# Filling projections in single steps, and the low weights of decay and rate over all rows

## The chip, the cores and the metric

The kernel runs on one core of a Trainium2 chip. The time is the device time of one execution in microseconds (us). A core has four engines that compute: TensorE (PE in the rows; its weight loads are PEld), VectorE (DVE), ScalarE (ACT) and GpSimd (POOL); SyncE (SP) and ScalarE issue most DMAs. Every engine works through its own queue in order and waits where a result of another engine is missing.

## What is computed

One step of a streaming encoder layer, for 1024 new prompt rows and 64 sample rows of width 1024. One input projection feeds two groups of heads. Group A is differential attention (8 heads, a block-causal mask of 64 rows). Group B is an RWKV-7 recurrence (16 heads of 64), whose decay and learning rate come from a projection of rank 64:

```python
proj = h @ w_in
...
w_log = -jax.nn.softplus(-(w0 + jnp.tanh(wd) @ w_up)) - 0.5
decay = jnp.exp(-jnp.exp(w_log))
a = jax.nn.sigmoid(a0 + ad @ a_up)
...
s = s * w_t + sa * b_t + v_t * k_t          # per row t, s is 64x64 per head
...
out = mix @ w_out
x_new = x + _rms_norm(out, norm_post, NORM_EPS)
```

Both groups are gated, joined and sent through one output projection; keys, values, the recurrent state and the last shifted row are returned as well.

## The kernel before

Matrix products of the projections are done as three products of a high and a low part each: weights and activations are split into a rounded high part (`wh`, `hhi`) and the rest (`wl`, `hlo`), and high by high, high by low and low by high are added in PSUM.

The work is cut into *streams*, Python generators that emit instructions and yield. `Weave` decides whose turn it is: it keeps a clock of its own (`now`, moved by `spend` for work of TensorE), each stream says when it may go on (`yield ns`), and the stream of the lowest rank that is due goes first. This fixes the order in every engine's queue; at run time nothing is chosen.

Group B has 17 units, two for each of 8 head pairs (named 0_0, 0_1, 1_0 ... 7_1 in the rows) and one for the sample rows (None_2). A unit first makes decay and rate (`up` products, L513 and L514, into `m_up`), inverts a triangular matrix per chunk in five levels (`m_ip` L684, VectorE L688, `m_iq` L694, VectorE L698 and L703), and then goes through 8 chunks in a chain, one after another: L804 (`pt`) gives a product that VectorE copies (L818, `gsb`), L821 uses it and VectorE copies the result (L827, L828), L832 (`bkt`) updates the state, and VectorE (L842) makes the next chunk's start of it. Beside the three stand L809 or L824 and L833, which sum the output `y`.

Units have ranks 0 to 16. The *filling* has rank 100 and runs when no unit is due. It is first the input projection, in jobs of 128 columns (`proj_cm`): 32 jobs feed the units (r, k, v, g of the 8 pairs) and 32 the attention (aq, ak, av, ag of 8 heads), plus one for decay and rate. A job has three chunks of 384, 384 and 320 rows, each of 24 matmuls into one PSUM tile `pj`: for each of 8 parts of the inner width the three products, L215, L216, L217. It may be interrupted after every third. Of the attention's jobs at least six are held back for the attention. After them the filling is the output projection (`po`, L1145 to L1147), in groups of four by three matmuls of 512 columns, again interrupted after every third.

The attention's streams have ranks from 0 to 80. Per head, `prep` loads queries, keys, values and the gate, splits them, and per 128 query rows come scores (`s`, L1322 and L1323), maximum, exponential, transposes (`x_wt`) and the sum (`x_o`). Keys and queries of four heads at a time are turned by `rope` (rank above 50), in 8 steps that go through DRAM. What is left of the output projection runs alone behind the attention.

For the `up` products, `xw` holds tanh of the decay's activations: the high part in rows 0 to 63 and the low part in rows 64 to 127; `xa` holds the rate's the other way round. The tile `t` holds w_up and a_up twice, in both row halves, their high parts in `t[:, 0:2]` and their low parts in `t[:, 2:4]`. The first of two matmuls takes the high weights by all 128 rows, the second the low weights by the 64 rows of the high activations.

## Time and profile before

| | |
|---|---|
| median of 3 runs | 1876.28 us (1874.08 to 1876.33) |
| the profiled execution | 1870.95 us |
| its span, first to last instruction | 1869.1 us |
| TensorE busy | 1699.6 us (91%) |
| VectorE busy | 1305.8 us (70%) |
| ScalarE, GpSimd busy | 868.1, 695.4 us |
| granted TensorE clock, mean | 0.975 of full |

A matmul's length in a timeline contains its way through the array; where several follow each other, the distance of their starts tells what one costs. Group B ends at 1236 us of the span, the attention at 1746 us.

### The profile page before, as it was taken

How to read it: one execution, taken by the hardware profiler on the slowest of the kernel's cores; microseconds unless marked ns; L12 is line 12 of the kernel's file. 1: busy time of each engine (PE TensorE's matmuls, PEld its weight loads, DVE VectorE, ACT ScalarE, POOL GpSimd, SP SyncE). 2: the span in 40 equal slices, each digit the busy share in tenths (PEclk: the TensorE clock that was granted, in tenths of full speed). 3: DMA queues.
4: the chain of work that ended last, by engine and by line, in shares of the span. 5: the costliest groups of instructions: out<-in, count | busy, mean ns of one | idle time of the engine just before them, and what ended most of it. 6: DMA issues, size and time to landing. Idle time of an engine off the chain costs nothing. (4 is left out here: it accounts for less than half of the span.)

```text
span 1869.1 us, 34871 instructions
## 1 busy us (share of the span) xinstructions
PE 1699.6 (91%) x12930; PEld 1500.6 (80%) x12930; DVE 1305.8 (70%) x2892; ACT 868.1 (46%) x2155; POOL 695.4 (37%) x866
## 2 busy tenths in 40 slices
PE   6999899999998999999999899977899798889995
PEld 5888888888888888888888789877778676777784
DVE  5568777777778787886875766524687667787336
ACT  5534444344344444444443433323566576676323
POOL 4442333233233323323332421212332356554657
PEclk9999999999999999999999999998999899899998
DMA  4110111321122111110101121345555565443325
GB/s 144 49 55 27 50 48 48 80 82 36 39 72 62 51 44 35 52 38 29 57 26 50 57 62 50 106 118 160 153 156 149 165 155 156 121 131 105 116 87 181
DMA packets 204244, 158.85 MB, mean 85 GB/s; under 512 B 44229, under 2 KB 185194, under 8 KB 204074
## 3 DMA queue, kind: packets, MB, share of 16 engines
q1 hardware_dynamic: 169242, 137.33, 25.5%
q10 hardware_dynamic: 34832, 19.30, 4.0%
q8 instruction: 102, 1.67, 0.4%
q14 instruction: 68, 0.56, 0.1%
HBM read 108.67 MB, written 47.34 MB: 83 GB/s over the span
## 5 line engine op out<-in xcount | busy, mean ns | idle before, releaser
L1348 ACT ACTIVATE e<-s,nb 128x512 f32<-128x512 f32 (+4 forms) x208 | 117.3, 569 | 59.3 <-DVE nb L1332 26.1
L1145 PE MATMUL po<-woh,mxh 128*128 128x512 f32 x288 | 120.3, 419 | 7.1 <-DVE part L1156 5.9
L1147 PE MATMUL po<-wol,mxh 128*128 128x512 f32 x288 | 115.9, 402 | 3.9 <-DVE nb L1337 2.5
L1146 PE MATMUL po<-woh,mxl 128*128 128x512 f32 x288 | 115.5, 401 | 4.2 <-POOL mxl L158 4.2
L1332 DVE TENSOR_REDUCE nb<-s 128x1 f32<-128x512 f32 (+4 forms) x208 | 108.0, 529 | 15.9 <-PE s L1323 14.6
L158 POOL TENSOR_TENSOR mxl<-mxr,mxh 128x512 fp32r<-128x512 f32 (+1 forms) x72 | 88.3, 1231 | 74.9 <-ACT mxh L157 61.8
L811 ACT ACTIVATE sd<-suv,dc 64x64 f32<-64x64 f32 x128 | 44.4, 347 | 154.1 <-DVE suv L842 149.4
L1322 PE MATMUL s<-k,qs 128*128 128x512 f32 (+4 forms) x208 | 78.9, 385 | 22.0 <-ACT k L1249 10.0
L1395 PE MATMUL x_o<-vn,wt 128*128 128x128 f32 (+1 forms) x608 | 88.0, 289 | 10.1 <-DVE wt L1385 5.4
L1395 PEld LDWEIGHTS x_o<-vn,wt 128*128 128x128 f32 (+1 forms) x608 | 81.0, 200 | 18.5 <-issue 5.5
L1156 DVE TENSOR_TENSOR part<-po,part 128x512 f32<-128x512 f32 x72 | 49.5, 688 | 55.6 <-PE po L1147 55.5
L842 DVE SCALAR_TENSOR_TENSOR suv<-cbank,dc,sd 64x64 f32<-64x64 f32 x224 | 63.0, 281 | 33.3 <-PE cbank L832 29.2
L832 PE MATMUL cbank<-suv,bkt 128*128 128x128 f32 x256 | 56.9, 304 | 32.0 <-DVE suv L828 32.0
L832 PEld LDWEIGHTS cbank<-suv,bkt 128*128 128x128 f32 x256 | 41.1, 190 | 45.7 <-DVE suv L828 43.4
L215 PE MATMUL pj_v<-hhi,wh_v 128*128 128x384 f32 (+1 forms) x192 | 70.1, 365 | 6.5 <-DVE mg L416 6.1
L1409 POOL TENSOR_SCALAR ms<-ms 128x1 f32<-128x1 f32 x72 | 18.0, 249 | 150.9 <-ACT osq L1407 150.4
L1323 PE MATMUL s<-k,qs 128*128 128x512 f32 (+4 forms) x208 | 71.5, 358 | 2.4 <-POOL k L1252 1.5
L215 PE MATMUL pj_av<-hhi,wh_av 128*128 128x384 f32 (+1 forms) x192 | 70.2, 365 | 3.0 <-DVE fl_g L939 3.0
L157 ACT CAST mxh<-mxr 128x512 fp32r<-128x512 f32 (+1 forms) x72 | 40.7, 567 | 68.7 <-PE po L1147 29.4
L677 POOL TENSOR_TENSOR ltlo<-lt,lt 64x512 f16<-64x512 f32 x32 | 37.7, 1177 | 93.4 <-ACT lt L665 92.2
L1145 PEld LDWEIGHTS po<-woh,mxh 128*128 128x128 f32 x288 | 55.4, 192 | 20.6 <-DVE part L1156 4.4
L215 PE MATMUL pj_k<-hhi,wh_k 128*128 128x384 f32 (+1 forms) x192 | 67.7, 352 | 4.0 <-ACT raw_k L230 4.0
(533 smaller groups left out, 6189.5 us busy)
## 6 DMA issues: line engine op xcount, KB each, us to landing
mxr<-mixB SPq DMA_DIRECT2D x32, 256.0 KB
wor<-in_w_out SPq DMA_DIRECT2D x64, 128.0 KB
qa<-scr_q SPq DMA_DIRECT2D x32, 204.0 KB
ka<-scr_k SPq DMA_DIRECT2D x32, 204.0 KB
scr_q<-fl_q SPq DMA_DIRECT2D x8, 544.0 KB
scr_k<-fl_k SPq DMA_DIRECT2D x8, 544.0 KB
scr_v<-fl_v SPq DMA_DIRECT2D x8, 544.0 KB
scr_g<-fl_g SPq DMA_DIRECT2D x8, 544.0 KB
```

Source lines behind the costliest of these rows:

```text
L158: gtt(lo, raw, hi.bitcast(F32), op=SUB)
L215: mm(ps[:, :n], hi[:, k, :], hhi[i][:, k, :], start=(k == 0), stop=False)
L832: mm(s, bkt[:, c], suv[:, c], start=True, stop=True)
L842: stt(suv[r, c + 1, h, :] if c < 7 and not smp else to[r], s[r, h * CH:(h + 1) * CH], dc[r, c:c + 1], sd[r], op0=MUL, op1=ADD)
L1145: mm(ps, hi[:, q, :], wh, start=(q == 0), stop=False)
L1146: mm(ps, lo[:, q, :], wh, start=False, stop=False)
L1147: mm(ps, hi[:, q, :], wl, start=False, stop=(q == len(ks) - 1))
L1322: mm(s[:, 0:w], lq, k1[c][:, k0 + o_:k0 + o_ + w], start=True, stop=False)
L1323: mm(s[:, 0:w], lq, k2[c][:, k0 + o_:k0 + o_ + w], start=False, stop=True)
L1332: nc.vector.tensor_reduce(nb[:, i_:i_ + 1], s[:, 0:w], axis=AX.X, op=MAX, negate=True)
L1348: act(e[:, o_:o_ + w], s[:, 0:w], AF.Exp, bias=mx, accum_out=sm)
L1395: mm(ops[:, 0:P], wt[0:w, b, :], vn[0:w, vb, :], start=(b == 0), stop=(b == len(kbs) - 1))
```

## The change

`proj_cm` yields after each of the 24 matmuls instead of each third, and spends a third as much of Weave's clock each time; so does the output projection. The constant `QK`, which was 1, goes, and the start of the program takes three steps of the first job where it took one. In the `up` products the second matmul takes all 128 rows of the low weights and the activations instead of 64, so that the low weights are multiplied by the low activations too. Line numbers move: L215 to L217 are L216 in the changed kernel, L1145 to L1147 are L1147, and L513, L514 stay.

```diff
--- before.py
+++ after.py
@@ -42,7 +42,6 @@
 LA, LAT, W_LD, W_DMA = 130, 100, 11000, 3122
 MB = 3
 W_L0 = 22000
-QK = 1
 DVE, ACT, POOL = "DVE", "ACT", "POOL"
 RS = 1.0
 RATE = {DVE: 1 / 0.96, ACT: 1 / 1.2, POOL: 2.4}
@@ -212,12 +211,12 @@
         for i, (t0, n) in enumerate(TCH):
             ps = pjp.tile([P, 512], F32, tag="pj", name=f"pj_{tag}_{i}")
             for k in range(KC):
-                mm(ps[:, :n], hi[:, k, :], hhi[i][:, k, :], start=(k == 0), stop=False)
-                mm(ps[:, :n], hi[:, k, :], hlo[i][:, k, :], start=False, stop=False)
-                mm(ps[:, :n], lo[:, k, :], hhi[i][:, k, :], start=False, stop=(k == KC - 1))
-                weave.spend(3 * n / 2.4 + 60)
-                if k < KC - 1 and k % QK == QK - 1:
-                    yield 0
+                for j, (a, b) in enumerate(((hi, hhi), (hi, hlo), (lo, hhi))):
+                    last = k == KC - 1 and j == 2
+                    mm(ps[:, :n], a[:, k, :], b[i][:, k, :], start=(k == j == 0), stop=last)
+                    weave.spend(n / 2.4 + 20)
+                    if not last:
+                        yield 0
             evac(ps[:, :n], t0, n)
             yield 0
 
@@ -252,7 +251,7 @@
                 gk = pc(R_NP + k)
                 act(hhi[g][:, k, :], ps[:, :w], AF.Copy, scale=gk)
                 stt(hlo[g][:, k, :], ps[:, :w], gk, hhi[g][:, k, :].bitcast(F32), op0=MUL, op1=SUB)
-                if g > 0 and k % QK == QK - 1:
+                for _ in range(3 if g > 0 else 0):
                     next(first[1])
             if g == 0:
                 raw, evac = raw_rows("wa")
@@ -507,11 +506,12 @@
                     d = op_(POOL, 256)
                 yield d
                 for q, t in enumerate(ups):
-                    for j, (x, r) in enumerate(((xw, slice(0, 64)), (xa, slice(64, 128)))):
+                    for j, x in enumerate((xw, xa)):
                         o_ = pss2[j][:, (q0 + q) * CH:(q0 + q + 1) * CH] if smp else pss2[j]
                         cl = slice(TP, T) if smp else slice(hf * HALF, (hf + 1) * HALF)
+
                         mm(o_, t[:, j], x[:, cl], start=True, stop=False)
-                        mm(o_, t[r, 2 + j], x[r, cl], start=False, stop=True)
+                        mm(o_, t[:, 2 + j], x[:, cl], start=False, stop=True)
                 spend(900)
 
             sq = t512(nm=f"sq{u}")
@@ -1142,12 +1142,12 @@
             ps = pjp.tile([P, 512], F32, tag="pj", name=f"po{g}{tt}{ch}")
             for q, k in enumerate(ks):
                 wh, wl = ws[g][k, ch]
-                mm(ps, hi[:, q, :], wh, start=(q == 0), stop=False)
-                mm(ps, lo[:, q, :], wh, start=False, stop=False)
-                mm(ps, hi[:, q, :], wl, start=False, stop=(q == len(ks) - 1))
-                spend(690)
-                if q < len(ks) - 1:
-                    yield 0
+                for j, (a, b) in enumerate(((hi, wh), (lo, wh), (hi, wl))):
+                    last = q == len(ks) - 1 and j == 2
+                    mm(ps, a[:, q, :], b, start=(q == j == 0), stop=last)
+                    spend(230)
+                    if not last:
+                        yield 0
             p_ = part[tt][:, ch * 512:(ch + 1) * 512]
             if g in (0, 2):
                 nc.scalar.copy(p_, ps)
```

All orders below are TensorE's. Each row is line, operation, output, inputs and size; a number behind a name is a tile's own. The first place is the up products of unit 5_1 (`m_up5_1`), with the filling job av1 (or ag0) and the chain of unit 4_1 around it. Before:

```order
L217 MATMUL pj_av1_0_9238<-hhi0_173,wl_av1_9035 128x384
L513 MATMUL m_up5_10_9262<-xw_466,t_wus5_10_9264 128x512
L514 MATMUL m_up5_10_9262<-xw_466,t_wus5_10_9264 128x512
L832 MATMUL cbank_509<-suv4_1_8924,bkt4_1_8893 128x128
L833 MATMUL y4_10_9006<-suv4_1_8924,rbk4_1_8252 128x128
L513 MATMUL m_up5_11_9263<-xa_467,t_wus5_10_9264 128x512
L514 MATMUL m_up5_11_9263<-xa_467,t_wus5_10_9264 128x512
L215 MATMUL pj_av1_0_9238<-hhi0_173,wh_av1_9034 128x384
```

After:

```order
L216 MATMUL pj_ag0_0_9206<-hhi0_173,wh_ag0_9001 128x384
L513 MATMUL m_up5_10_9220<-xw_466,t_wus5_10_9222 128x512
L514 MATMUL m_up5_10_9220<-xw_466,t_wus5_10_9222 128x512
L513 MATMUL m_up5_11_9221<-xa_467,t_wus5_10_9222 128x512
L514 MATMUL m_up5_11_9221<-xa_467,t_wus5_10_9222 128x512
L216 MATMUL pj_ag0_0_9206<-hlo0_176,wh_ag0_9001 128x384
L216 MATMUL pj_ag0_0_9206<-hhi0_173,wl_ag0_9002 128x384
```

The four stand side by side after the change; before, the chain's L832 and L833 stood between the second and the third, as they did in the second units of pairs 2 to 6.

The second place is one chunk in the chain of unit 4_1, from L804 by L821 (input `gsb4_12`) to L832. Before:

```order
L804 MATMUL cbank_509<-suv4_1_8924,pt1_499 128x128
L809 MATMUL y4_10_9006<-suv4_1_8924,pt1_499 128x128
L215 MATMUL pj_v5_2_9170<-hhi2_175,wh_v5_8795 128x320
L216 MATMUL pj_v5_2_9170<-hlo2_178,wh_v5_8795 128x320
L217 MATMUL pj_v5_2_9170<-hhi2_175,wl_v5_8796 128x320
L215 MATMUL pj_v5_2_9170<-hhi2_175,wh_v5_8795 128x320
L216 MATMUL pj_v5_2_9170<-hlo2_178,wh_v5_8795 128x320
L217 MATMUL pj_v5_2_9170<-hhi2_175,wl_v5_8796 128x320
L821 MATMUL cbank_509<-gsb4_12_9187,xtf_504 128x128
L215 MATMUL pj_v5_2_9170<-hhi2_175,wh_v5_8795 128x320
L216 MATMUL pj_v5_2_9170<-hlo2_178,wh_v5_8795 128x320
L217 MATMUL pj_v5_2_9170<-hhi2_175,wl_v5_8796 128x320
```

After:

```order
L804 MATMUL cbank_509<-suv4_1_8653,pt1_499 128x128
L809 MATMUL y4_10_8702<-suv4_1_8653,pt1_499 128x128
L216 MATMUL pj_r5_0_8759<-hlo0_176,wh_r5_8401 128x384
L216 MATMUL pj_r5_0_8759<-hhi0_173,wl_r5_8402 128x384
L821 MATMUL cbank_509<-gsb4_12_8839,xtf_504 128x128
L216 MATMUL pj_r5_0_8759<-hhi0_173,wh_r5_8401 128x384
L216 MATMUL pj_r5_0_8759<-hlo0_176,wh_r5_8401 128x384
L216 MATMUL pj_r5_0_8759<-hhi0_173,wl_r5_8402 128x384
L216 MATMUL pj_r5_1_8869<-hhi1_174,wh_r5_8401 128x384
L832 MATMUL cbank_509<-suv4_1_8653,bkt4_1_8628 128x128
L833 MATMUL y4_10_8702<-suv4_1_8653,rbk4_1_8055 128x128
L568 MATMUL m_ib5_00_8871<-ident_79,t_inx5_0_8848 128x128 x4
```

Between L804 and L821 stood six filling matmuls and stand two; between L821 and L832 six and four.

The third place is the start of the attention: the transposes of the cached keys (`x_ck`) and the first scores of head 0 (`s0_000`). Before:

```order
L215 MATMUL pj_av4_2_15426<-hhi2_175,wh_av4_15152 128x320
L216 MATMUL pj_av4_2_15426<-hlo2_178,wh_av4_15152 128x320
L217 MATMUL pj_av4_2_15426<-hhi2_175,wl_av4_15153 128x320
L1232 MATMUL x_ck00_15518<-ident_79,ck0_15299 128x128
L1232 MATMUL x_ck01_15527<-ident_79,ck0_15299 128x128
L1322 MATMUL s0_000_15602<-k100_15557,qs00_15544 128x128
L1323 MATMUL s0_000_15602<-k200_15568,qs00_15544 128x128
```

After:

```order
L216 MATMUL pj_ak6_0_15146<-hlo0_176,wh_ak6_15033 128x384
L216 MATMUL pj_ak6_0_15146<-hhi0_173,wl_ak6_15034 128x384
L1232 MATMUL x_ck00_15170<-ident_79,ck0_14961 128x128
L1232 MATMUL x_ck01_15176<-ident_79,ck0_14961 128x128
L216 MATMUL pj_ak6_1_15182<-hhi1_174,wh_ak6_15033 128x384
L216 MATMUL pj_ak6_1_15182<-hlo1_177,wh_ak6_15033 128x384
L216 MATMUL pj_ak6_1_15182<-hhi1_174,wl_ak6_15034 128x384
...
L216 MATMUL pj_ak6_1_15182<-hlo1_177,wh_ak6_15033 128x384
L216 MATMUL pj_ak6_1_15182<-hhi1_174,wl_ak6_15034 128x384
L1322 MATMUL s0_000_15226<-k100_15194,qs00_15184 128x128
L1323 MATMUL s0_000_15226<-k200_15203,qs00_15184 128x128
```

Twelve filling matmuls now stand between the transposes and the first score. From the last instruction of group B (the transpose `shp`) to the first score it is 93 filling matmuls before and 135 after.

## Rows read from the trace of the kernel before

**Rows 1.** The page, part 1: busy time, share and instructions of each engine.

```profile
PE 1699.6 (91%) x12930; PEld 1500.6 (80%) x12930; DVE 1305.8 (70%) x2892; ACT 868.1 (46%) x2155; POOL 695.4 (37%) x866
```

**Rows 2.** Windows: a cycle of group B, and a stretch of the attention.

```profile
core 0: us, PE busy (x) PEld busy (x) DVE busy (x) ACT busy (x) POOL busy (x), PEclk, DMA share, GB/s
...
809.40:938.90 129.50, 123.60 (x1097) 110.93 (x1097) 100.56 (x214) 56.55 (x129) 42.87 (x53) 1.00 0.13 41
1516.00:1682.00 166.00, 147.04 (x846) 119.76 (x844) 131.05 (x323) 113.50 (x336) 89.76 (x108) 0.97 0.53 141
```

**Rows 3.** Waits of PE, 278 to 1067 us: total us, times, longest us.

```profile
PE cbank L832 <- DVE suv L828: 23.0, 29, 3.2
...
PE m_iq L694 <- DVE q L688: 2.6, 6, 0.6
```

**Rows 4.** Timeline of PE, unit 3_0's up matmuls: start, length, instruction.

```profile
417.53 0.47 PE L513 MATMUL m_up<-xw,t_wus 128*128 128x512 f32 x1
417.93 0.50 PE L514 MATMUL m_up<-xw,t_wus 64*128 64x512 f32 x1
418.36 0.50 PE L513 MATMUL m_up<-xa,t_wus 128*128 128x512 f32 x1
418.79 0.50 PE L514 MATMUL m_up<-xa,t_wus 64*128 64x512 f32 x1
419.22 0.45 PE L215 MATMUL pj_r<-hhi,wh_r 128*128 128x384 f32 x1
419.50 0.34 PE L216 MATMUL pj_r<-hlo,wh_r 128*128 128x384 f32 x1
419.68 0.34 PE L217 MATMUL pj_r<-hhi,wl_r 128*128 128x384 f32 x1
```

**Rows 5.** Timeline of PE in the tail: 512-column matmuls over 128 rows.

```profile
1800.16 0.39 PE L1145 MATMUL po<-woh,mxh 128*128 128x512 f32 x1
1800.39 0.39 PE L1146 MATMUL po<-woh,mxl 128*128 128x512 f32 x1
```

**Rows 6.** Line L514, its matmuls of the prompt units: count, shortest, median, longest.

```profile
L514 PE MATMUL m_up<-xw,t_wus x16: 492/502/502, 66.4 to 1076.6; 64*128 64x512 f32 x16
```

**Rows 7.** Timeline of PE: the sample unit's first batch, and four transposes.

```profile
1013.83 0.28 PE L513 MATMUL m_upNone<-xw,t_wusNone 128*128 128x64 f32 x1
...
1017.42 0.44 PE L215 MATMUL pj_av<-hhi,wh_av 128*128 128x384 f32 x1
...
1231.71 0.60 PE L906 MATMUL m_zt<-ident,ycp 128*128 128x128 f32 x4
```

**Rows 8.** Timeline of PE, start of the attention; idle time and releaser in brackets.

```profile
1250.38 0.31 PE L216 MATMUL pj_av<-hlo,wh_av 128*128 128x320 f32 x1
1250.52 0.30 PE L217 MATMUL pj_av<-hhi,wl_av 128*128 128x320 f32 x1
1252.24 0.41 PE L1232 MATMUL x_ck<-ident,ck 128*128 128x128 f32 x2 [1.42 <-DMA ck<-in_cache_k]
1262.67 0.47 PE L1322 MATMUL s<-k,qs 128*128 128x128 f32 x1 [10.02 <-ACT k L1249]
```

**Rows 9.** Timeline of PE and DVE, a chain step of unit 4_1.

```profile
743.30 0.38 PE L804 MATMUL cbank<-suv,pt 128*128 128x128 f32 x2
...
743.67 0.48 PE L651 MATMUL m_bo<-t_kbh,bdr 128*128 128x512 f32 x1
...
743.73 0.29 DVE L818 COPY gsb<-cbank 128x128 f32<-128x128 f32 x1 [0.81 <-PE cbank L804]
...
744.74 0.38 PE L821 MATMUL cbank<-gsb,xtf 128*128 128x128 f32 x2
...
745.68 1.25 DVE L369 SCALAR_TENSOR_TENSOR vs__491<-pv,vs__491 128x1 f32<-128x1 f32 x1
...
747.29 0.23 DVE L828 COPY suv<-cbank 64x64 f32<-64x64 f32 x1
747.57 0.49 PE L832 MATMUL cbank<-suv,bkt 128*128 128x128 f32 x2 [0.74 <-DVE suv L828]
```

## The prediction

> **What bounds the kernel now.** I read the page's busy shares first: TensorE is busy for 1699.6 of 1869.1 us [rows 1], far ahead of the next engine. Then the windows by stage. The kernel has three: the recurrent heads (group B, up to 1236 us) with the projections as filling, the attention (to 1746 us) with the last projections and the output projection as filling, and a tail of output projection alone. In group B the program repeats itself every 129.5 us, one head pair a cycle: in the cycle from 809.4 us TensorE is busy 123.6 of 129.5 us, VectorE 100.6 [rows 2]. In the attention stretch from 1516 us it is 147.0 and 131.1 of 166 us [rows 2]. So TensorE is the bound nearly everywhere, VectorE stands close behind, and the time of the kernel is TensorE's work plus what TensorE waits. The profile shows its waits in group B: between 278 and 1067 us the longest group by far is L832, the chain's state update, which waits 29 times for the copy L828, 23.0 us together and up to 3.2 us at once; the inversion's L694 waits 6 times, 2.6 us together [rows 3].
>
> The change touches both: it takes work from TensorE (the low part), and it moves where TensorE stands when it waits (the interruptions). The number of instructions is the same; only their order and the shape of 48 matmuls differ.
>
> **Part 1, the low part over all rows: -18 us.** Per unit four matmuls of 512 columns: full rows, 64 rows, full rows, 64 rows. In the trace they start at 417.53, 417.93, 418.36 and 418.79 us, the filling follows at 419.22: 1.69 us, some 0.43 us each once the shapes alternate, and the first filling matmul behind takes 0.28 us to its successor instead of 0.18 [rows 4]. Matmuls of 512 columns over 128 rows that follow each other start 0.23 us apart [rows 5]. So what costs is not the columns but the alternation, about 0.2 us at each step. With all four over 128 rows I expect 4 x 0.23 = 0.92 us and no surcharge behind: 1.79 - 0.92 = 0.87 us less per unit, and 16 prompt units [rows 6] make 13.9 us. The sample unit has 32 such matmuls of 64 columns in two batches of 16; a batch takes 1017.42 - 1013.83 = 3.59 us, 0.22 us each [rows 7]. No row shows a 64-column matmul of this type in a stream of its own kind; four 128-column transposes take 0.60 us with their drain [rows 7], so 0.15 us each is an upper bound: 16 x 0.15 = 2.4 us, 1.2 us saved per batch, 2.4 in all, and 7.2 if they cost nothing. Together 16.3 to 21.1; I take 18 us, nearer to the low end since a 64-column row has more overhead than columns. All of it lies on TensorE, which is 95% busy; it covers nothing now, so nothing is uncovered. If VectorE were the bound there, it would come back as idle time (a rival below). The added product (low weights by low activations) costs no instruction: POOL already writes the low weights of all rows (L506).
>
> The Trainium skill, "TensorEngine Tiling (Array Packing)", Key Properties, says that changing the tiling mode drains the engine; the trace agrees with 0.43 against 0.23 us [rows 4, 5]. The same section says that different row tiles can load and multiply in parallel, which speaks against the change: the two 64-row matmuls lie on different row halves and could share one's time, 16 x 0.23 = 3.7 us given up. They start 0.86 us apart with a full-row matmul between [rows 4], so there is nothing to give up; by that rule alone the sum would be 3.7 us worse.
>
> **Part 2, fewer other changes of row shape: -4 us.** In TensorE's order I counted the places where a 64-row matmul stands next to a 128-row one: 486 before, 96 of them at the up projection; 362 after, none of them due to it. The other 390 thus become 362. Such a place costs between 0.10 us (the 0.28 for 0.18) and 0.20 us (0.43 for 0.23) [rows 4]: 28 x 0.15 = 4 us, bounds 3 and 6.
>
> **Part 3, the start of the attention: -7 us.** At 1250.52 us the last filling matmul stands, then TensorE waits 1.4 us for the cache and 10.0 us for the cast of head 0's keys [rows 8]. That cast waits for loads, which start with the stage, not with the filling. Before, 93 filling matmuls stand between group B's last work and the first score, after 135, 12 of them behind the cache transposes (the third place in the order). 42 x 0.16 us, between the 0.18 us of 384 columns [rows 4] and the 0.14 of 320 [rows 8], is 6.7 us of work that now lies in the wait. Bounds: 0, if the loads come later by as much, and 11.4, the whole wait.
>
> **Part 4, the interruptions: +12 us, bounds -5 and +50.** A filling projection has 24 matmuls per chunk; a unit's work could stand behind every third, now behind each. What this does not change is the amount of filling: 4,680 + 864 matmuls. They are interrupted 778 times before and 802 times after, 7.1 and 6.9 matmuls from stop to stop. So the cover of an average step is as it was; it is divided otherwise. Before, 552 of the 778 runs are exactly 3, 6 or 9 matmuls long; after, 545 of 802 are 1 to 5. A step of the chain that got 6 by rounding up now gets 2 to 4, and the rest stands where the unit waits for its projections. Is that still enough? The shortest answer to L804 in the trace: it starts at 743.30, the copy L818 runs from 743.73 to 744.02, so 0.72 us; L804 and its companion L809 take 0.37 us to the next matmul, and two filling matmuls 2 x 0.17 more, 0.71 in all [rows 9]. Just covered. L821 to L832 needs L821's 0.38, two copies of 0.23 and handovers, about 1.0 us [rows 9]; four filling matmuls (the second place) and L821's own slot, half of the 0.37, give 0.9: short by 0.1. But where TensorE waits long now, it waits for VectorE's queue: behind L821 at 744.74 stands an L369 of 1.25 us ahead of the copies, so that they end at 747.52 us and L832 starts at 747.57 after 0.74 us idle, although eight matmuls lay between [rows 9]. Such waits are neither made nor mended by a finer grain. There are 17 units x (24 chain steps + 9 inversion steps) = 561 steps. If a fifth of them lack 0.1 us, as the second example does, that is 11 us; I take 12. Upper bound: one filling matmul, 0.17 us, on half of them, 48, taken as 50. Below nothing: the L832 that stands amid the up projection (the first place) stands elsewhere after, and its 0.74 us, five times over by the same place of five units, would be -4; with the few waits at L694 I call it -5. I take a value near the low end, because the plan knows VectorE's load, and where it leaves little cover today (L694, 6 waits [rows 3]) it waits little.
>
> In the attention the score-to-output order has nearly as many rows from the first score to the last output matmul, 2226 before and 2241 after. I take +3 us there, bounds 0 and the 19 us that TensorE is idle in the stretch of 166 us [rows 2]. With group B shorter in filling, projections move into the attention and output projection out of it: 441 of its matmuls stand behind the attention before, 629 after. These 188 run there at 0.23 us each [rows 5], 43 us of work that is taken from the stages ahead, so moving it costs nothing. With the filling move its weight loads on SP, their splits on ACT and POOL and its evacuations; only the rope below comes close to its use by that.
>
> Sum: -18 - 4 - 7 + 12 + 3 = -14 us on the profiled execution's 1870.95 us (span 1869.1 and 1.85 around it), 1857 us. That execution lies 5.3 us below the median of the three runs; a median is asked for, so 1876.3 - 14 = 1862 us.
>
> **Rivals.** *Late answers outweigh it (slower).* TensorE's queue is in order: a unit's matmul that is put behind one filling matmul instead of three stops all filling when VectorE's copy is not there. Parts 1 to 3 give 29 us; over 802 stops that is 36 ns each, so a mean added wait over 36 ns, a fifth of one filling matmul, turns the sign. For it: 1.0 us needed against 0.9 given at L832, where the longest waits are already; VectorE at 78% in the cycle, rising if the cycle shrinks. Against it: 7.1 and 6.9 matmuls per stop. At the upper bound: 1876.3 - 29 + 50 = 1897 us, with 0.1 us on all 561 steps 1876.3 - 29 + 56 = 1903. In the same case I count the rope of the keys of heads 4 to 7: its last step now stands beside the last scores of head 3, where before it stood at the start of head 2, and a late load would stop the scores of head 4 as it stops head 0 today, 10 us [rows 8]. Chance 0.24.
>
> *VectorE or the chain is the bound in the cycle (same).* Then parts 1 and 2 come back as idle time and parts 3 and 4 cancel: within 4 us of 1876. For it: VectorE's 100.6 of 129.5 us and its in-order queue; against it: TensorE's 123.6. Chance 0.12.
>
> *The units gain and nothing is lost.* Part 4 at its lower bound, part 1 at 22: 1876.3 - 38 = 1838 us. It is the low edge of the forecast's case, which has 0.64 in all.
>
> **How the numbers follow.** Forecast 1862 us, 0.64. A measurement of this kernel tells 0.2%, 3.8 us, from no change. Faster by more: 0.64; within: 0.12; slower: 0.24. The range leaves out one tenth at each side: down to 1842 (part 4 at nothing, part 3 at its bound, attention at 0), up to 1890 (the first rival short of its upper bound).
>
> **What would show it.** Right: the four up matmuls about 0.23 us apart and the cycle about 2 us shorter; the wait for head 0's cast near 3 us; L832's waits in sum as before. Wrong: more TensorE waits of 0.1 to 0.3 us at L821, L832, L694 and L684; a wait at head 4's first score; or a cycle that stays at 129.5 us with VectorE's share as before. If the time falls much below 1842, waits vanish that I hold to be VectorE's own.

## The result and the profile after

The changed kernel takes 1936.19 us (median of 4 runs, 1930.36 to 1937.15), the kernel before 1875.18 in the same comparison: 1.0324 times as long, interval 1.0296 to 1.0353. The change makes the kernel slower by some 61 us. The profiled execution has a span of 1928.6 us where before had 1869.1.

The page of the changed kernel, part 1, answers to [rows 1]; below it, from the view by cores, span and mean granted clock of TensorE (0.975 before):

```profile
PE 1719.9 (89%) x12930; PEld 1510.3 (78%) x12930; DVE 1299.7 (67%) x2892; ACT 866.7 (45%) x2155; POOL 688.8 (36%) x866
```

```profile
core 0: 1928.6 us, clock 0.960
```

The 59.5 us more of span split in two. TensorE idles 208.7 us instead of 169.5, 39.2 more. And it is busy 20.3 us longer, with as many instructions and less work in them: the second part of the loss is the clock, below.

By stage the trace gives: group B ends at 1224.3 us (1235.6 before), 11.3 us earlier with 234 filling matmuls fewer in it; from there to the first score 32.3 us (27.0); the attention 506 us (483); the tail 43 us more, for the 188 output matmuls that the prediction saw move there.

In group B's steady part TensorE has the same instructions in each cycle before and after, 432 of them filling. The windows: the cycle of the changed kernel that answers to [rows 2], then four cycles together, in the changed kernel and in the kernel before.

```profile
core 0: us, PE busy (x) PEld busy (x) DVE busy (x) ACT busy (x) POOL busy (x), PEclk, DMA share, GB/s
705.30:839.80 134.50, 125.52 (x1096) 111.64 (x1095) 100.10 (x216) 56.27 (x128) 41.59 (x53) 0.99 0.13 41
434.80:973.70 538.90, 503.07 (x4380) 447.26 (x4379) 403.03 (x873) 225.24 (x512) 166.70 (x211) 0.98 0.16 47
417.50:939.00 521.50, 495.31 (x4384) 443.78 (x4382) 405.34 (x874) 226.41 (x513) 170.52 (x209) 1.00 0.16 47
```

The cycle is 5.0 us longer, not 2 shorter; VectorE's time in it is unchanged. Of the 17.4 us in four cycles 9.6 are idle time and 7.8 more busy time.

TensorE's waits in the stretch of [rows 3], in the changed kernel: total us, times, longest us.

```profile
PE m_iq L694 <- DVE q L688: 15.8, 7, 3.1
PE cbank L821 <- DVE gsb L818: 11.5, 17, 1.4
PE cbank L804 <- DVE suv L842: 10.7, 16, 1.0
PE m_ip L684 <- DVE x L703: 5.4, 8, 2.3
PE cbank L832 <- DVE suv L828: 5.3, 7, 1.0
```

In the kernel before, beside the rows of [rows 3]:

```profile
PE cbank L821 <- DVE gsb L818: 5.8, 6, 1.8
PE m_ip L684 <- DVE x L703: 0.4, 2, 0.2
```

L832, the longest group before, has fallen from 23.0 to 5.3 us. L694 has grown from 2.6 to 15.8, and L821, L804 and L684, at which the prediction's sum had at most 0.1 us here and there, wait 27.6 us together, where L821 and L684 had 6.2 and L804 was not among the waits. The waits went to the steps that were covered before, or nearly so.

**Where the answer comes late: one chunk.** Timeline of PE and DVE, two chunks of a chain just ahead of the up products of unit 3_0, the place of [rows 4]; idle time and releaser in brackets:

```profile
432.20 0.39 PE L832 MATMUL cbank<-suv,bkt 128*128 128x128 f32 x2
...
432.42 1.26 DVE L966 TENSOR_TENSOR raq<-raq,rbq 128x136 f32<-128x136 f32 x1
...
433.17 0.34 PE L216 MATMUL pj_r<-hhi,wh_r 128*128 128x384 f32 x1
433.71 0.60 DVE L842 SCALAR_TENSOR_TENSOR suv<-cbank,dc,sd 64x64 f32<-64x64 f32 x2
434.37 0.49 PE L804 MATMUL cbank<-suv,pt 128*128 128x128 f32 x2 [0.86 <-DVE suv L842]
...
434.83 0.48 PE L513 MATMUL m_up<-xw,t_wus 128*128 128x512 f32 x1
435.15 0.39 PE L514 MATMUL m_up<-xw,t_wus 128*128 128x512 f32 x1
435.38 0.40 PE L513 MATMUL m_up<-xa,t_wus 128*128 128x512 f32 x1
435.62 0.39 PE L514 MATMUL m_up<-xa,t_wus 128*128 128x512 f32 x1
```

Between L833 and L804 stand four filling matmuls, some 0.7 us. The answer L842 stands on VectorE behind a rope step of 1.26 us (L966), and TensorE is idle for 0.86 us. Before, six stood at this place and sixteen small products of an inversion (L694), and L804 did not wait. The last four rows show part 1 as forecast: 0.23 us apart behind the first.

**And what a wait costs behind it.** TensorE and VectorE, an inversion level of the changed kernel:

```profile
616.86 0.34 PE L216 MATMUL pj_ak<-hlo,wh_ak 128*128 128x384 f32 x1
...
618.64 0.69 DVE L875 TENSOR_TENSOR ycp<-ycp,gva 128x512 f32<-128x512 f32 x1 [2.05 <-POOL gva L873]
619.25 0.68 DVE L688 TENSOR_TENSOR q<-m_ip,mt 128x512 f16<-128x512 f32 x1
...
619.99 0.63 PE L694 MATMUL m_iq<-xt_a,q 64*64 64x64 f16 x16 [2.79 <-DVE q L688]
...
621.04 0.52 PE L216 MATMUL pj_ak<-hhi,wh_ak 128*128 128x384 f32 x1
621.36 1.05 PE L906 MATMUL m_zt<-ident,ycp 128*128 128x128 f32 x4
```

Windows ahead of, in and behind this wait (columns as above):

```profile
613.00:616.80 3.80, 3.55 (x31) 3.23 (x30) 3.56 (x7) 2.05 (x4) 2.89 (x4) 1.00 0.46 132
616.80:619.90 3.10, 0.40 (x3) 0.08 (x1) 1.26 (x3) 0.00 (x0) 1.96 (x3) 0.82 0.09 21
619.90:624.50 4.60, 4.51 (x31) 4.27 (x32) 2.66 (x6) 1.56 (x3) 2.03 (x2) 0.50 0.00 0
624.50:630.00 5.50, 5.50 (x52) 4.90 (x51) 5.44 (x10) 2.59 (x6) 1.69 (x2) 0.90 0.07 20
```

L688 stands on VectorE right behind L875, which waits 2.05 us for GpSimd; six filling matmuls cover 1.0 us, and TensorE idles 2.79. Then the granted clock is 0.50, the lower of its two levels (1.2 against 2.4 GHz), for 4.6 us, and a filling matmul of 384 columns takes 0.32 us to its successor (621.04 to 621.36) where it takes 0.17 elsewhere. So this wait costs 2.8 us at once and, by an estimate of half the 4.5 busy us at 0.50, 2.3 more behind it. The same wait comes back at 485.87, 757.74 and 891.63 (2.80, 2.79 and 2.79 us), with a granted clock of 0.61 to 0.64 over the 4.2 to 4.8 us from there. Over the whole span busy time by the share of clock not granted is 1719.9 x 0.040 = 69 us after and 1699.6 x 0.025 = 42 us before: an estimate of 26 us for the clock's part in the loss. To be explained are some 32: the 20.3 us of busy time, and the 11.5 by which the low part over all rows shortens it when it stands alone (first experiment). What makes the other 6 is not shown.

### The profile page after: what moved, and what is told of

Same layout as the page of the kernel before. It is cut to its first block, busy times and chain, and to the rows that moved or that the text cites. A ratio compares the mean times of both kernels' runs of the same rounds, so it can differ in the third digit from the quotient of the medians.

```text
span 1928.6 us, 34957 instructions
## 1 busy us (share of the span) xinstructions
PE 1719.9 (89%) x12930; PEld 1510.3 (78%) x12930; DVE 1299.7 (67%) x2892; ACT 866.7 (45%) x2155; POOL 688.8 (36%) x866
## 4 chain that ended last, share of the span: by engine, by line
PE 52%; DVE 20%; POOL 8%; ACT 7%; DMA 6%; issue 5%; ACTq 1%; SPq 1%; POOLq 0%; DVEq 0%
PE po L1147 8%; PE pj_aq L216 4%; PE pj_av L216 4%; PE pj_v L216 3%; PE pj_r L216 3%; PE pj_ak L216 3%; PE pj_k L216 3%; PE pj_g L216 3%; PE cbank L821 2%; PE pj_ag L216 2%; PE cbank L804 2%; PE cbank L832 2%; PE x_o L1395 2%; PE m_s L633 2%; POOL inv L547 1%
## 5 line engine op out<-in xcount | busy, mean ns | idle before, releaser
L1348 ACT ACTIVATE e<-s,nb 128x512 f32<-128x512 f32 (+4 forms) x208 | 117.2, 569 | 63.5 <-DVE nb L1337 32.4
L1147 PE MATMUL po<-woh,mxh 128*128 128x512 f32 x288 | 117.1, 407 | 7.0 <-DVE part L1156 5.9
L1147 PE MATMUL po<-wol,mxh 128*128 128x512 f32 x288 | 116.8, 406 | 0.6 <-POOL wol L157 0.5
L1147 PE MATMUL po<-woh,mxl 128*128 128x512 f32 x288 | 116.0, 403 | 1.1 <-POOL mxl L157 1.1
L1381 PE MATMUL x_wt<-ident,e 128*128 128x128 f32 (+1 forms) x304 | 55.1, 296 | 32.1 <-DVE e L1370 9.4
L842 DVE SCALAR_TENSOR_TENSOR suv<-cbank,dc,sd 64x64 f32<-64x64 f32 x224 | 63.1, 282 | 30.1 <-PE cbank L832 25.7
L1409 POOL TENSOR_SCALAR ms<-ms 128x1 f32<-128x1 f32 x72 | 22.0, 305 | 163.7 <-ACT osq L1407 163.3
L688 DVE TENSOR_TENSOR q<-m_ip,mt 128x512 f16<-128x512 f32 x80 | 55.2, 690 | 30.9 <-PE m_ip L684 29.8
L821 PE MATMUL cbank<-gsb,xtf 128*128 128x128 f32 x256 | 58.5, 310 | 16.5 <-DVE gsb L818 16.3
L1381 PEld LDWEIGHTS x_wt<-ident,e 128*128 128x128 f32 (+1 forms) x304 | 38.2, 149 | 43.7 <-ACT on L1403 10.0
L1147 PEld LDWEIGHTS po<-woh,mxh 128*128 128x128 f32 x288 | 55.5, 193 | 21.2 <-DVE part L1156 4.5
L216 PE MATMUL pj_k<-hhi,wh_k 128*128 128x384 f32 (+1 forms) x192 | 67.4, 351 | 4.3 <-ACT raw_k L229 4.3
L804 PE MATMUL cbank<-suv,pt 128*128 128x128 f32 x256 | 59.0, 313 | 12.9 <-DVE suv L842 12.1
```

Of the source, the lines that this page charges most:

```text
L216: mm(ps[:, :n], a[:, k, :], b[i][:, k, :], start=(k == j == 0), stop=last)
L804: mm(g, pt[:, c, 0:2, :], suv[:, c], start=True, stop=True)
L821: mm(uu, xtf[:, c], gsb, start=True, stop=True)
L842: stt(suv[r, c + 1, h, :] if c < 7 and not smp else to[r], s[r, h * CH:(h + 1) * CH], dc[r, c:c + 1], sd[r], op0=MUL, op1=ADD)
L1147: mm(ps, a[:, q, :], b, start=(q == j == 0), stop=last)
L1348: act(e[:, o_:o_ + w], s[:, 0:w], AF.Exp, bias=mx, accum_out=sm)
```

## The experiments

Intervals are of the ratio to the kernel before, measured beside it. `LAT` (100 ns, group B) and `LA` (130 ns, attention) of line 42 are the planner's allowance: it adds them to the time at which it takes an answer to be there, so they decide how much filling it puts behind a step. A chain step has two such stops: one until VectorE's copy is issued, and one until the next product.

### The three parts alone

**Low part over all rows.**

```diff
-                    for j, (x, r) in enumerate(((xw, slice(0, 64)), (xa, slice(64, 128)))):
+                    for j, x in enumerate((xw, xa)):
...
-                        mm(o_, t[r, 2 + j], x[r, cl], start=False, stop=True)
+                        mm(o_, t[:, 2 + j], x[:, cl], start=False, stop=True)
```

> The kernel before with the low part over all rows alone; the order of all instructions is that of before. Theory A (part 1 of the prediction holds, the loss is all from the finer interruptions): 18 us of TensorE work less, the four matmuls about 0.23 us apart, 1875 - 18 = 1857 us, 1852 to 1862. Rival B (the saved TensorE time comes back as waits, since VectorE or the chain is the bound of a cycle): 1871 to 1876 us, the cycle stays at 129.5 us. Rival C (full rows are dearer than I think and are part of the loss): over 1876 us.

Measured: 1867.77 us, 0.9973 (0.9959 to 0.9987), -5 us: between the theories. The order is that of before. From the first up matmul to the instruction behind the last, the 16 prompt units sum to 24.0 us instead of 32.4; the sample unit's first batch is

```profile
1010.10 0.28 PE L513 MATMUL m_upNone<-xw,t_wusNone 128*128 128x64 f32 x1
...
1011.89 0.42 PE L215 MATMUL pj_av<-hhi,wh_av 128*128 128x384 f32 x1
```

1.79 us instead of 3.59 [rows 7]. The second gains nothing (4.88 us, 4.82 before), and the rows show why: it stands behind a wait of 3.13 us at L832 and runs at a granted clock of 0.50, its matmuls 0.21 us apart instead of the first batch's 0.11, where before no such wait stood ahead of it and it ran at 1.00. The windows of the second batch, here and in the kernel before (columns as above):

```profile
1023.00:1028.00 5.00, 4.37 (x20) 3.83 (x18) 2.35 (x6) 2.33 (x6) 2.71 (x4) 0.50 0.01 2
1026.80:1031.70 4.90, 3.96 (x19) 3.02 (x18) 2.75 (x6) 2.33 (x6) 2.63 (x4) 1.00 0.01 2
```

So 10.2 us are saved, and 1.6 more on the first matmul behind each of the units; TensorE is busy 1688.1 us, 11.5 less than before. More than half comes back as waits: over 66 to 1236 us, where before had 32.0 us at L832 (36 times) and 7.7 at L821 (9 times), this kernel has

```profile
PE cbank L832 <- DVE suv L828: 36.5, 36, 3.2
PE cbank L821 <- DVE gsb L818: 10.9, 13, 1.8
```

**Grain of the input projections.**

```diff
...
-                weave.spend(3 * n / 2.4 + 60)
-                if k < KC - 1 and k % QK == QK - 1:
-                    yield 0
...
+                    weave.spend(n / 2.4 + 20)
+                    if not last:
+                        yield 0
...
```

> The kernel before with the input projections alone interruptible at each matmul; low part over 64 rows, output projection by thirds. Theory A (answers of VectorE come late in group B and in the attention's first half, where these projections are the filling): most of the loss, 1876 + 45 to 65 = 1920 to 1940 us. Rival B (the loss comes from the attention with the output projection as filling): 1876 to 1890 us.

Measured: 1938.02 us, 1.0355 (1.0340 to 1.0371): theory A. It is the whole loss, 65 us, with the cycles of the changed kernel (134.5 us).

**Grain of the output projection.**

```diff
...
-                spend(690)
-                if q < len(ks) - 1:
-                    yield 0
...
+                    spend(230)
+                    if not last:
+                        yield 0
...
```

> The kernel before with the output projection alone interruptible at each matmul. Group B is then as before, word for word. Theory A: the score's and sum's answers come late in the second half of the attention, +5 to +20 us, 1880 to 1895 us. Rival B (the attention's loss in the changed kernel comes from the keys' rope of heads 4 to 7 and from the shifted projections, not from the grain): 1871 to 1879 us.

Measured: 1869.12 us, 0.9987 (0.9972 to 1.0002): no change, against theory A and just below rival B's range. The attention falls from 483 to 470 us, and 44 output matmuls go to the tail, 10 us. The loss in the attention is not from this part.

### Cover given back, and taken away without the grain

**The changed kernel with more allowance.**

```diff
-LA, LAT, W_LD, W_DMA = 130, 100, 11000, 3122
+LA, LAT, W_LD, W_DMA = 310, 280, 11000, 3122
```

> The changed kernel, with two constants of the plan raised by 180 ns each: LAT from 100 to 280 (group B) and LA from 130 to 310 (attention), the time that the plan adds to each answer. 180 ns is half of what a stop came later on average when a third was the grain (half of 540 against half of 180 ns). 4067 filling matmuls then stand in group B (4083 before, 3849 in the change), 493 output projection matmuls behind the attention (441 and 629). Theory A (a finer grain took away a cover that the plan's short answer times needed): the waits at L804, L821, L684 and L694 in group B fall back to the 14 us of before, and the time to 1855 to 1870 us. Rival B (being interrupted so often costs by itself, whatever the cover: row shapes, weight loads, clock): it stays at 1915 us or more. Rival C (the place of the later jobs, the rope of heads 4 to 7 above all, does it): group B recovers half, the attention stays at 500 us or more, 1890 to 1910 us.

Measured: 1875.18 us, 1.0013 (0.9994 to 1.0031). The loss is gone, though every projection can still be interrupted at each matmul (830 interruptions, 802 in the changed kernel), and four cycles take 519.3 us. That is theory A's mechanism, 5 us above its range: the gain of the low part does not come on top, and the waits at its four lines do not fall back to the 14 us of before. From 66 to 1236 us they are 54 us in the changed kernel and 27 here. Waits from 278 to 1067 us:

```profile
PE cbank L832 <- DVE suv L828: 18.3, 17, 3.4
PE cbank L821 <- DVE gsb L818: 8.0, 12, 1.4
...
PE cbank L804 <- DVE suv L842: 6.9, 6, 1.3
PE m_iq L694 <- DVE q L688: 2.9, 3, 1.4
```

Between the kernel before and the changed one it is the division of the same 432 filling matmuls of a cycle that differs. I counted two steps in TensorE's order, for all 17 units:

| filling matmuls | before | changed | more allowance |
|---|---|---|---|
| L804 to L821: mean | 9.9 | 6.2 | 8.6 |
| of 136, with three or fewer | 22 | 67 | 25 |
| L684 to L694: mean | 6.3 | 4.8 | 5.6 |
| of 85, with five or fewer | 14 | 69 | 40 |

**In group B alone (`LAT` 280), in the attention alone (`LA` 310), and half of both (190, 220).**

> The changed kernel with the allowance per step raised from 100 to 280 ns in group B alone; in the attention it stays at 130 ns. The run with both raised took 1875 us, the changed kernel 1936. Theory A (cover is lost in each stage by itself; by the stage times 36 us of the loss stand in group B and 20 to 25 in the attention): 1893 to 1905 us, with group B back near 1230 us. Theory B (the loss in the attention is a consequence of group B, from which 234 filling matmuls were pushed out into it): 1873 to 1883 us. Theory C (the attention is the larger part): above 1912.

> The changed kernel with the allowance raised from 130 to 310 ns in the attention alone; in group B it stays at 100 ns. Theory A (each stage loses by itself): the attention from first score to last output matmul falls from 506 to some 480 us and the time to 1905 to 1918 us. Theory B (the attention's loss comes from the projections that group B pushes into it): 1928 to 1940 us, no change. Group B itself should be as in the changed kernel, 1224 us, in both.

> The changed kernel with both allowances raised half as far (190 in group B, 220 ns in the attention). A dose: if each nanosecond of cover is worth the same, half of the 61 us comes back, 1900 to 1910 us. If only the last bit of cover up to the answer matters and most steps are just short (a threshold), 1875 to 1890 us; if the steps lack more than half of it, above 1915.

Measured: 1886.64 us, 1.0071 (1.0047 to 1.0094); 1929.00, 1.0289 (1.0264 to 1.0314); 1880.54, 1.0044 (1.0029 to 1.0059). Of the 61 us (by the ratios) group B's allowance alone gives back 47, between the two theories. It also takes the attention from 506 to 474 us, of which the filling that no longer stands there (192 input matmuls fewer, 76 output ones more) explains about 13, an estimate at 0.16 and 0.23 us each. The attention's allowance alone gives back 7, too little for theory A and in theory B's range. Half of both gives back 52, as the threshold reading expects: most of what was missing lay within the first 90 ns of a stop. Why the attention loses when group B is thin stays partly open; that more of the input projections are left for it (696 matmuls instead of 504) is seen in the order, but no run moved those alone.

**The kernel before with less allowance** (`LAT` 2, thirds as before).

```diff
-LA, LAT, W_LD, W_DMA = 130, 100, 11000, 3122
+LA, LAT, W_LD, W_DMA = 130, 2, 11000, 3122
```

> The kernel before, still interrupted at thirds only, with the planner's allowance per step of a unit in group B cut from 100 to 2 ns, so that the order puts 117 fewer filling matmuls into group B (3966 where 4083 stood; the changed kernel has 3849). Theory A (what hurts is the missing cover behind the steps, however it is taken away): slower by about half of what the changed kernel loses in group B, 1890 to 1910 us, with more waits at L804, L694 and L684. Theory B (the single-matmul interruptions themselves hurt, by broken runs of filling, and not the amount of cover): 1870 to 1882 us.

Measured: 1912.90 us, 1.0209 (1.0190 to 1.0227): theory A, somewhat over its range. L821 to L832 now has three or fewer filling matmuls 44 times instead of 20, and four steady cycles take 534 us (521.5). From 278 to 1067 us the waits at L821 are 11.9 us (5.8 before), at L694 5.6 (2.6) and at L684 4.7 (0.4); L804, which theory A names too, has 1.2. The fine grain is not needed for a loss.

**Longer durations instead of a longer allowance** (the changed kernel, `RS = 1.2`, by which the planner multiplies work of VectorE, ScalarE and GpSimd).

> The changed kernel with the planner's durations of work on VectorE, ScalarE and GpSimd raised by a fifth, the allowance per step left at 100 and 130 ns. It gives cover by the length of the work that is waited for, where the raised allowance gave the same to every step. Theory A (the plan's durations were too short, and the thirds' rounding made up for it): 1860 to 1880 us, no worse than the raised allowance's 1875. Theory B (what lacked is the handover of each step, which no duration holds): 1885 to 1915 us.

Measured: 1903.52 us, 1.0166 (1.0148 to 1.0184): theory B. It gives back 30 of the 61 us (by the ratios). Longer durations help the steps with long work: L684 to L694, with 512 columns to mask, has five or fewer 33 times instead of 69. L804 to L821, where 128 columns are copied, still has three or fewer 54 times (67).

**More allowance with thirds** (low part over all rows, `LAT` 200).

> The kernel before with the low part over all rows and the allowance in group B raised from 100 to 200 ns, interruptions at thirds; 105 filling matmuls more than before then stand in group B (4188). The full-row form alone took 1868 us. Theory A (its saving came back as waits because cover was missing, and more cover frees it): 1852 to 1863 us, with shorter waits at L832 and L821. Theory B (cover at thirds was enough; what comes back is the chain's own time): 1866 to 1876 us.

Measured: 1894.72 us, 1.0108 (1.0087 to 1.0129), outside both theories. Four cycles take 538 us, with 33 more filling matmuls (some 6 us), and the waits at L832 hardly shrink (30.5 us over 66 to 1236). More allowance is thus no cure in itself. Counted as above, it did not come to every step: L804 to L821 has three or fewer 38 times (22 before) and L821 to L832 31 times (20), while L832 to the next L804 within a chain has 8.3 on the mean instead of 5.4. That this division is the cost is not shown.

### One place, or many

**The order on VectorE.** In the changed kernel L688 stands right behind L875 (at most two others between) in six places, before in none, and with the raised allowance in none. Is that order the loss?

```diff
+            nrm[0] = True
             yield op_(DVE, 512)
...
             yield op_(DVE, 512)
+            nrm[0] = False
...
             for lv in range(1, 6):
+                yield lambda: not nrm[0]
```

> The changed kernel, with a gate: an inversion level's first product (m_ip) is not issued while an output normalisation stands between its sum of squares and its scaling. It takes away one place that comes back in each head pair of the changed kernel: on VectorE the level's masking stands right behind the normalisation's scaling, which waits 2.05 us for GpSimd, and TensorE then idles 2.79 us and goes on at a lower clock. The filling in group B stays thin (3868 matmuls; 3849 in the changed kernel, 4083 before). Theory A (this order on VectorE is most of the longer cycle): the cycle falls from 134.5 us to 129 to 131 and group B is 20 to 30 us shorter, 1905 to 1918 us in all. Theory B (thin cover everywhere is the loss, this place only one of many): the cycle stays above 133 us, 1925 to 1940 us.

Measured: 1926.64 us, 1.0292 (1.0254 to 1.0331): theory B by the time. But the gate did not take all six places away. Three are left (at 349.6, 487.9 and 1031.5 us; the scaling is L878 and the masking L690 here), and the inversion's product has longer waits than in the changed kernel: 4.96 us at 488.61 and 4.42 at 627.30. The counts of the table stay thin (63 of 136, 66 of 85). Waits from 278 to 1067 us (lines are two higher here):

```profile
PE cbank L823 <- DVE gsb L820: 13.5, 13, 3.4
PE m_iq L696 <- DVE q L690: 11.0, 5, 5.0
PE cbank L806 <- DVE suv L844: 8.2, 12, 1.5
PE cbank L834 <- DVE suv L830: 7.9, 9, 2.4
```

So the whole time does not decide between the theories. Two cycles in which the place is gone tell more; here they are together, and the same two in the changed kernel and in the kernel before (columns as above):

```profile
704.70:970.30 265.60, 247.10 (x2197) 220.81 (x2196) 199.64 (x428) 114.06 (x259) 83.99 (x107) 1.00 0.13 40
705.30:973.70 268.40, 251.03 (x2191) 223.24 (x2190) 199.64 (x429) 112.69 (x256) 82.94 (x105) 0.99 0.13 40
679.80:939.00 259.20, 247.28 (x2193) 221.77 (x2192) 201.13 (x427) 113.11 (x257) 85.70 (x105) 1.00 0.13 41
```

A cycle takes 132.8 us without the place, 134.2 with it and 129.6 before. So the place is worth some 1.4 of the 4.6 us that a cycle lost, and theory B is the nearer one. The rest stays as waits at other steps, 7.7 us at L823 alone; that the gate makes none of them is not shown. Without the two waits of 2.79 us TensorE is at full clock and busy 3.9 us less with the same work. The estimate above, 2.3 us of slower work behind each such wait, gives 4.6.

### Whether TensorE's time counts, and the best version

**No low-weight matmuls at all** (the second of each pair left out; that part of the computation is missing).

```diff
-                        mm(o_, t[:, j], x[:, cl], start=True, stop=False)
-                        mm(o_, t[r, 2 + j], x[r, cl], start=False, stop=True)
+                        mm(o_, t[:, j], x[:, cl], start=True, stop=True)
```

> The kernel before without the low-weight matmuls of decay and rate (the second matmul of each pair, 32 of 512 columns and 16 of 64, left out; that part of the computation is missing). It takes from TensorE some 1.2 us per unit and all changes of row shape there, about 22 us in all, where the full-row form alone took about 14 to 18 and gave 5. Theory A (TensorE's time in group B is worth its full length unless a wait needs it): 1851 to 1860 us. Theory B (the chain's answers set the cycle there, so that time taken from this place comes back as waits at L832 and L821): 1862 to 1870 us, no better than the full-row form by more than 4 us.

Measured: 1857.46 us, 0.9929 (0.9907 to 0.9951): in theory A's range, though not at its full length. The up matmuls take some 24 us less of TensorE, group B ends 17 us earlier, and 13 us (by the ratio) to 16 (by the medians) reach the end. Four cycles take 517.2 us instead of 521.5, with 7.0 us less busy time. So the chain alone does not set the cycle: somewhat over half of what is saved comes through, and the rest comes back as waits.

**The two harmless parts together.**

> Two of the three parts of the change: the low part over all rows and the output projection interrupted at each matmul; the input projections at thirds as before. Alone they measured 0.9973 and 0.9987 of the kernel before. If they add up: 0.995 to 0.997, 1863 to 1868 us. If the finer output projection costs cover in the attention as the finer input projections do in group B, or only moves work to the tail: 1868 to 1876 us.

Measured: 1864.27 us, 0.9955 (0.9941 to 0.9969), -8.4 us: the two add up (0.9973 x 0.9987 = 0.9960). This version beats both kernels.

```profile
PE 1686.2 (91%) x12930; PEld 1498.0 (80%) x12930; DVE 1302.0 (70%) x2892; ACT 865.8 (47%) x2155; POOL 691.7 (37%) x866
```

TensorE is busy 13.4 us less than before [rows 1].

## Why the prediction was wrong, step by step

**The bound: right, and not whole.** TensorE's work plus its waits was the right frame, and TensorE's time does count (the run without low-weight matmuls). Missing was that a long wait also slows the work behind it: 39.2 us of idle time came with 20.3 us of busy time.

**Part 1, -18 us: direction right, about 5 us.** The four matmuls stand 0.23 us apart as forecast. But the step multiplied 0.87 us by all units. Measured in the first experiment are 0.53 us on the mean and 0.10 on the first matmul behind, which the 0.87 held too: the first of the four took 0.33 to 0.40 us before, not 0.43, and where the chain's L832 and L833 stand amid the four (five units of the kernel before, as the first place of the order showed) the gain is 0.3 us. The sample unit gave 1.8 us, once, instead of 2.4, since its second batch fell on the lower clock. That makes 11.8 us, and the sentence that the time "covers nothing now" failed for more than half of it: it stood between steps of other units' chains, and came back at L832 and L821.

**Part 2, -4 us: not told apart.** No run separates it.

**Part 3, -7 us: at its bound of 0.** Timeline of the changed kernel, start of the attention:

```profile
1247.06 0.34 PE L216 MATMUL pj_ak<-hhi,wl_ak 128*128 128x384 f32 x1
...
1255.37 1.20 ACT L1249 CAST k<-ka 128x1216 fp32r<-128x1216 f32 x1 [2.33 <-DMA rot_k<-fl_k]
1256.63 0.47 PE L1322 MATMUL s<-k,qs 128*128 128x128 f32 x1 [9.23 <-ACT k L1249]
```

The wait for head 0's cast is 9.23 us, 10.02 before [rows 8], where the prediction expected near 3. The 42 matmuls more did not lie in the wait; the stage became 5.3 us longer, nearly their 6.7 us. The loads came later by as much, the case that the lower bound held. The first load of the keys, before and in the changed kernel:

```profile
1253.97 0.37 SPq L1206 DMA_DIRECT2D ka<-rot_k  x1
1248.75 0.30 SPq L1206 DMA_DIRECT2D ka<-rot_k  x1
```

It is issued 18 us behind the end of group B before and 24 us after, so the loads do not start with the stage. What holds them is not shown.

**Part 4, +12 us: this step failed.** The input projections' grain costs 65 us by itself. The working was: as many matmuls per interruption (7.1 and 6.9), hence the cover of an average step is as it was. The first half is right: each steady cycle has 432 filling matmuls before and after. The second is not, because a wait is not paid by the average. L804 to L821 lost 3.7 matmuls on the mean, and the steps with three or fewer went from 22 to 67 of 136; what they lost stands between the chain of one unit and that of the next, where the prediction had put it ("where the unit waits for its projections"): from a unit's last L832 to the next unit's first L804 it is 960 filling matmuls in all instead of 639. Within the chains L832 to L804 has about as much as before, 6.0 on the mean and 5.4. The prediction looked at L804 to L821 once, found 0.71 us given and 0.72 needed, and called it covered; a distribution counted in the order would have shown it. The rounding up to thirds was a hidden allowance of about 0.17 us at each stop, an estimate: half of three matmuls against half of one, at 0.17 us each. The runs with `LAT` and `LA` agree: put back, the loss is gone; taken from the kernel with thirds, a loss is there.

Two reasons in that step fell. That waits behind VectorE's queue "are neither made nor mended by a finer grain" is contradicted by L832 (23.0 to 5.3 us) and by L694 and L804, whose new waits stand behind L875 and L966 in that queue. And the upper bound of 50 us took one filling matmul on half of the steps, with no room for the clock.

**Attention, +3 us: 23 measured.** The waits from the first score to the last output matmul grew, at changing lines; idle time there is 78 us instead of 57, at a clock of 0.92 instead of 0.95. The windows after and before (columns as above):

```profile
1257.00:1762.00 505.00, 426.92 (x2560) 369.30 (x2560) 338.14 (x900) 286.55 (x868) 190.04 (x247) 0.92 0.50 136
1263.00:1746.00 483.00, 426.31 (x2559) 363.82 (x2559) 347.92 (x903) 296.51 (x888) 209.89 (x268) 0.95 0.52 142
```

The 188 matmuls that went to the tail "cost nothing" only if the stages ahead become shorter by their 43 us. They did not: group B became 11 us shorter and the attention 23 longer. The moved work is the form in which the loss appears, since cover that is not used before the tail is worked off alone there.

**The rivals.** The first had the right mechanism, late answers behind an in-order queue, at too small a price (1897 and 1903 us). Its second half, a wait at the first score of head 4, did not come: that score starts at 1539.53 us without a wait. The second, VectorE or the chain as the bound, had the way in which part 1 came back by more than half; as the bound of the cycle it is refuted by the run without low-weight matmuls, and its time by the 61 us.

## What to carry to other kernels

Where a planner puts filling behind steps in an in-order queue, the coarse unit of the filling is part of the cover: a finer unit takes half of the difference of the two units from every stop, so raise the planner's allowance by as much, or leave the grain. Judge such a change by the distribution of cover over the steps that wait, counted in the order, not by its mean, and book work that moves to an empty tail as a cost until a stage ahead is seen to shrink. Price a wait on TensorE as long as the 2.8 us seen here with the matmuls behind it at the lower clock.

## What had not been expected of the hardware

A wait of 2.79 us on a TensorE that was at full clock ahead of it was followed by 4.6 us at a granted clock of 0.50, in which 384-column matmuls stood 0.32 us apart instead of 0.17. In four cycles with the same instructions TensorE was busy 503.1 us instead of 495.3, although some of its work had become shorter. In two of these cycles without such waits (the gated kernel) it was busy as long as before.

Matmuls of 64 columns over 128 rows that follow each other start 0.11 us apart (16 from 1010.10 to 1011.89 us in the first experiment), where the alternation with 64-row ones took 0.22 [rows 7], both at a granted clock of 1.00: for small matmuls too the change of row shape costs as much as the matmul.
